# A recurrence of 64x64 products: units of two head groups, four quarters of the array, and outputs turned 128x128

## The chip, the cores and the metric

The kernel runs on one core of a Trainium2 chip. Its time is device microseconds (us) of one execution, the median of several runs. In what follows PE is TensorE's matmul side and PEld its weight loads; DVE is VectorE, ACT ScalarE, POOL GpSimd, SP SyncE, whose queue issues most DMAs.

## What is computed

The reference is two transformer blocks over 256 tokens of width 2048, all in float32. The first is an attention and convolution mixer with a gated feed-forward layer; the second has an "even" layer (another attention and a pooling branch) and an "odd" layer. The change touches the odd layer, and the first microseconds of the program.

The odd layer is a recurrence with a matrix state per head (32 heads of width 64):

```python
def step(state, inp):
    r_t, w_t, k_t, v_t, kk_t, a_t = inp
    sa = jnp.einsum('bhvk,bhk->bhv', state, -kk_t)
    state = (state * w_t[:, :, None, :]
             + sa[..., None] * (kk_t * a_t)[:, :, None, :]
             + v_t[..., None] * k_t[:, :, None, :])
    return state, jnp.einsum('bhvk,bhk->bhv', state, r_t)
```

Its inputs r, w, k, v, kk and a come from products of the shifted and mixed tokens with 2048x2048 weights (`od_w_r`, `od_w_k`, `od_w_v`) and two low-rank pairs. What it gives out is normalised per head, gets a bonus term, is multiplied by silu of a fourth product (`od_w_g`), and goes through `od_w_o`; a layer norm follows.

## The kernel before

Every large product streams its weights from HBM in pieces of 512 KB (`split_w`): one DMA on SP's queue into one of four buffers `wraw`, a ScalarE copy rounds it to the high part `wh` (L149), VectorE subtracts to get the low part `wl` (L151), and TensorE makes three products of high and low parts. `ws` (L168 to L170) has the tokens as the moving side, 24 matmuls of 256 columns a piece; `ts` (L187 to L189) has the weights moving, 12 matmuls of 512 columns a piece. Up to three pieces are fetched and split ahead.

After each piece `tick` is called. It takes items from queues that `spread` has filled, at a rate of items by ticks, so that all smaller work goes into the instruction streams between the pieces. When the program is built, a scheduler puts each engine's instructions into their final order from this order and the dependences, so that a step may move past a neighbour; `issue_after` adds an edge that it keeps. On the chip each engine takes its stream in order.

The recurrence is done in chunks of 64 tokens. The 32 heads are four groups j of eight heads; a group's pair index p (four pairs) and half h2 (two) name a head, with half h2 on partitions 0 to 63 or 64 to 127 (`HALF`). One `unit(j, c)` is one group and one chunk, 16 in all, each a list of steps which `slots` puts at places relative to a time t, the even and the odd group one place apart:

- `load_rows`: four DMAs of POOL's queue bring the factors from the spill in DRAM (L1343, tile `unit`); `load_values`: two of ACT's queue.
- `gram` (L1360): eight products with 64 rows, 128 columns, 128 moved columns, then two masking multiplies on VectorE (L1362).
- `pre`: eight 32x32 products (L1373) for the inverse of a triangular 64x64 block, and eight 64x64 products with the values (L1381).
- `join` (L1390): eight more 32x32 products; and the bonus on POOL (L1396).
- `seq_s` (L1404): eight 64x64 products with the state, where there is one (not in the first chunk).
- `seq_u`: four 128x128 transposes (L1412, copied by ScalarE, L1414; not in the last chunk), and eight 64x64 products that solve (L1417).
- `seq_o`: products that update the state (L1426, not in the last chunk) and that give the output (L1436, and L1440 with the state); four ScalarE copies bring the output out of PSUM (L1446).
- `norm`, `norm2`: the head norm, on ScalarE, VectorE and POOL (powers in `rpow`).

All these products are plain float32, which the profile shows as two records each. A step of one group is one PSUM bank of a ring of four (`aux`); it is emitted as pairs p with h2 inside, with the output half fixed by h2:

```python
PAIRS = [(h2, HALF[h2], HALF[1 - h2], p) for p in range(4) for h2 in range(2)]
...
for h2, hs, os, p in PAIRS:
    nc.tensor.matmul(ps[hs, p], st["ar"][hs, p, col[h2]], S[hs, p], start=True, stop=True)
```

The partitions of the operands choose the rows of the array and those of the output its columns, so this step uses two quarters of the 128x128 array, rows 0 to 63 with columns 0 to 63 and rows 64 to 127 with columns 64 to 127. Steps with `os` for one side use the two crossed quarters.

The queue of slots starts with the fourth v product, runs through the 32 pieces of the g products, and ends in the first half of the o products. Ahead of it, during the k products, `k_post` prepares each group's factors; its `blocks` (L1181) makes 16 64x64 products a call, in two calls a group, and `store_m` writes the masked 32x32 blocks to DRAM. `inverse` inverts them on VectorE, and `load_inverses` brings them back (L1320, tiles `xn`), four DMAs a group on SP's queue. `output(k)` turns the recurrence's output back with four transposes of 64-row pieces (L1504) for each of 16 tiles k.

At the program's start `mixer` builds six of the 16 token tiles (`to_fm`, transposes at L246, ScalarE copies at L316) before its first large product; the x pieces and the first weight pieces alternate on SP's queue.

Of the kernel before, what the change touches and what calls it, by code (L numbers as in the profile page):

```python
# [8 lines left out]
F32 = mybir.dt.float32  # L9
# [5 lines left out]
P = 128  # L15
# [22 lines left out]
class Mega:  # L38
# [116 lines left out]
    def ws(self, W, col0, X, evac):  # L155
# [110 lines left out]
    def constants(self):  # L266
# [9 lines left out]

        src = a["vecs"]
# [77 lines left out]
    def mixer(self):  # L355
# [537 lines left out]
    def odd(self, normed):  # L893
# [209 lines left out]
        def k_post(j, kr, kk, first):  # L1103
# [71 lines left out]
            def blocks(cp):  # L1175
                def go():
                    ps = self.aux().rearrange("p (u s) -> p u s", u=8)
                    for u in range(8):
# [3 lines left out]
                    st["mt", cp] = mt = kp.tile([P, 8, CH], F32, tag="mt", name="mt", bufs=2)  # L1182
                    nc.vector.tensor_tensor(out=mt, in0=ps, in1=gmask[:, 0, 0:CH].unsqueeze(1).broadcast_to((P, 8, CH)),
                                            op=ALU.mult)
                return go


            def store_m(cp):
                def go():
                    for h2 in range(2):  # L1190
                        for b in range(2):
                            o = h2 * 64 + b * 32
                            nc.sync.dma_start(
                                out=md[j // 2][j % 2, h2, b, cp * 8:cp * 8 + 8].rearrange("u s t -> s u t"),
                                in_=st["mt", cp][o:o + 32, :, b * 32:b * 32 + 32])
# [16 lines left out]
            def store_b():  # L1212
# [5 lines left out]
                    put(1, 0, lambda: st["r"]), put(0, 0, lambda: st["at"]), gains_k, blocks(0),  # L1218
                    put(0, 1, lambda: kk), row_k, blocks(1), wait, store_m(0), store_m(1)], [bonus, last, store_b]
# [82 lines left out]
        def r4(tag, name, shape=(4, CH), bufs=4):  # L1302
            return rp.tile([P, *shape], F32, tag=tag, name=name, bufs=bufs)

        def bank(n=CH):
            return self.aux()[:, :4 * n].rearrange("p (u s) -> p u s", s=n)

        def bc4(x):
            return x.unsqueeze(2).broadcast_to((P, 4, CH))


        PAIRS = [(h2, HALF[h2], HALF[1 - h2], p) for p in range(4) for h2 in range(2)]
        state = [None] * NG
# [9 lines left out]
        def unit(j, c):  # L1323
# [5 lines left out]
            def load_rows():  # L1329

                with self.tc.issue_after(seen["k"].ins):
                    load_factors()

            def load_factors():
                w = g8([P, 2048], "unit")
                st["ar"] = w[:, 0:512].rearrange("p (n s) -> p n s", n=4)
                st["bk"] = w[:, 512:1024].rearrange("p (n s) -> p n s", n=4)
                st["G"] = w[:, 1024:].rearrange("p (h n s) -> p h n s", h=2, n=4)

                d = w[:, 0:1024].rearrange("p (tn s) -> p tn s", s=P)  # L1340
                for h2, hs in enumerate(HALF):
                    for role in range(2):
                        nc.gpsimd.dma_start(  # L1343
                            out=d[hs, :, col[h2 ^ role]],
                            in_=spill[j][hs, c // 2, role].rearrange("p t n c s -> p (t n) c s")[:, :, c % 2])

            def load_values():

                st["Z"] = Z = r4("Z", "Z", (2, 4, CH))
                v = vall[c % 2 * CH:c % 2 * CH + CH, c // 2, j * 512:j * 512 + 512]  # L1350
                for h2 in range(2):
                    nc.scalar.dma_start(out=Z[HALF[1 - h2], h2],
                                        in_=v.rearrange("t (n h s) -> t h n s", n=4, h=2)[:, h2])

            def gram():
                ar, bk, G = st["ar"], st["bk"], st["G"]
                pss = [bank(P) for _ in HALF]
                for p in range(4):
                    for h2, hs in enumerate(HALF):
                        nc.tensor.matmul(pss[h2][:, p], bk[hs, p], ar[hs, p], start=True, stop=True)  # L1360
                for h2, ps in enumerate(pss):
                    nc.vector.tensor_tensor(out=G[:, h2], in0=ps, op=ALU.mult,  # L1362
                                            in1=gmask[:, h2].unsqueeze(1).broadcast_to((P, 4, P)))

            def pre():

                G, Z = st["G"], st["Z"]
                X = xn[j % 2][:, 4 * c:4 * c + 4]
                ps = bank(32)
                st["T"] = r4("Tm", "Tm", (4, 32), bufs=2)  # L1370
                for h2, hs, os, p in PAIRS:
                    o = 64 * h2
                    nc.tensor.matmul(ps[o + 32:o + 64, p], G[o:o + 32, h2, p, o + 32:o + 64], X[o:o + 32, p, 0:32],  # L1373
                                     start=True, stop=True)
                for o in (32, 96):
                    nc.vector.tensor_copy(st["T"][o:o + 32], ps[o:o + 32])
                st["X"] = r4("Xt", "Xt", bufs=2)
                nc.vector.transpose(st["X"].rearrange("p u s -> p (u s)"), X.rearrange("p u s -> p (u s)"))
                ps = bank()
                for h2, hs, os, p in PAIRS:  # L1380
# [349 lines left out]
```

## Time and profile before

| | before |
|---|---|
| median of 3 runs | 2441.2 us |
| lowest and highest run | 2435.44, 2445.77 us |
| profiled execution, its own time | 2436.61 us |
| its span in the profile | 2434.8 us |
| instructions | 39170 |
| PE, PEld, DVE, ACT, POOL busy | 2372.7, 2072.3, 1515.6, 1214.4, 223.4 us |
| TensorE clock granted, mean | 0.991 |
| HBM traffic over the span | 183 GB/s |

The span is that of one profiled execution, by the hardware profiler. Matmuls overlap in the records, so a busy PE is not one at its peak: the distance from one start to the next says what a matmul costs in a stream. A row "x16" of the timeline merges 16 records in a row; its first number is the first one's start, its second the time from there to the last one's end.

### The profile page before, as it was taken

To read this page: it belongs to the slowest core of one execution; us is meant where nothing else is said; L and a number is where in the kernel's file an instruction comes from. 1 tells how busy PE (TensorE), PEld (TensorE's weight loads), DVE (VectorE), ACT (ScalarE), POOL (GpSimd) and SP (SyncE) were. 2 spreads that over 40 slices of the span, in tenths; PEclk is the share of its full clock that TensorE was granted. 3 is DMA by queue.
4 is the path that set the end of the run, shared out by engine and by line. 5 is a ranking of instruction groups with operands and counts; after the bars stand their busy time and mean duration, and the time that the engine had idled before them with its cause. 6 is when DMAs were issued, how large, how long until landed. Compare 5 with 4: busy or idle time off the path is not lost.

```text
span 2434.8 us, 39170 instructions
## 1 busy us (share of the span) xinstructions
PE 2372.7 (97%) x15385; PEld 2072.3 (85%) x15385; DVE 1515.6 (62%) x2093; ACT 1214.4 (50%) x1937; POOL 223.4 (9%) x343
## 2 busy tenths in 40 slices
PE   8999999999999999999999999999999998999997
PEld 8998888788788888888888898999889996789975
DVE  5688888565654454454444544555587678885656
ACT  5433564444544444444344444564387765455662
POOL 0000200100000000000000000320000013145411
PEclk9999999999999999999999999999999999999998
DMA  7666656556566666666666556455666688866665
GB/s 230 196 185 192 175 170 189 160 185 203 160 191 190 190 190 185 191 191 190 193 194 191 168 184 190 149 164 182 196 189 194 185 238 232 220 169 157 149 169 135
DMA packets 287912, 451.18 MB, mean 185 GB/s; under 512 B 57903, under 2 KB 85103, under 8 KB 287727
## 3 DMA queue, kind: packets, MB, share of 16 engines
q1 hardware_dynamic: 263488, 428.50, 59.9%
q10 hardware_dynamic: 21167, 11.79, 1.8%
q0 software_dynamic: 3072, 8.39, 1.6%
q8 instruction: 121, 1.98, 0.3%
q14 instruction: 64, 0.52, 0.1%
HBM read 428.74 MB, written 17.77 MB: 183 GB/s over the span
## 4 chain that ended last, share of the span: by engine, by line
PE 78%; issue 7%; DVE 6%; DMA 4%; ACT 3%; POOL 1%; SPq 0%; ACTq 0%; DVEq 0%; POOLq 0%
PE acc L187 17%; PE acc L188 17%; PE acc L189 17%; PE acc L168 7%; PE acc L169 7%; PE acc L170 7%; DVE wl L151 2%; DMA wraw<-in_od_w_v 1%; ACT wh L149 1%; DMA wraw<-in_od_w_g 1%; DMA wraw<-in_od_w_k 0%; DMA inv<-md 0%; PE aux L246 0%; PE aux L659 0%; DVE xk L65 0%
## 5 line engine op out<-in xcount | busy, mean ns | idle before, releaser
L151 DVE TENSOR_TENSOR wl<-wraw,wh 128x1024 fp32r<-128x1024 f32 x762 | 935.1, 1228 | 752.8 <-ACT wh L149 750.0
L149 ACT ACTIVATE wh<-wraw 128x1024 fp32r<-128x1024 f32 x762 | 805.9, 1058 | 1004.4 <-PE acc L189 644.6
L187 PE MATMUL acc<-wh,xk 128*128 128x512 f32 x1520 | 599.6, 395 | 1.8 <-ACT kr L1226 1.3
L188 PE MATMUL acc<-wl,xk 128*128 128x512 f32 x1520 | 595.2, 392 | 5.4 <-DVE wl L151 5.3
L189 PE MATMUL acc<-wh,xk 128*128 128x512 f32 x1520 | 594.9, 391 | 0.0
L168 PE MATMUL acc<-xk,wh 128*128 128x256 f32 x1920 | 550.3, 288 | 0.5 <-ACT rr L1069 0.5
L169 PE MATMUL acc<-xk,wh 128*128 128x256 f32 x1920 | 544.5, 284 | 0.0
L170 PE MATMUL acc<-xk,wl 128*128 128x256 f32 x1920 | 540.8, 284 | 0.6 <-DVE wl L151 0.6
L168 PEld LDWEIGHTS acc<-xk,wh 128*128 128x128 f32 x1920 | 369.4, 193 | 4.4 <-ACT rr L1069 0.9
L169 PEld LDWEIGHTS acc<-xk,wh 128*128 128x128 f32 x1920 | 370.0, 193 | 0.4
L170 PEld LDWEIGHTS acc<-xk,wl 128*128 128x128 f32 x1920 | 367.5, 192 | 1.6 <-DVE wl L151 1.2
L188 PEld LDWEIGHTS acc<-wl,xk 128*128 128x128 f32 x1520 | 286.0, 188 | 65.3 <-DVE wl L151 7.5
L187 PEld LDWEIGHTS acc<-wh,xk 128*128 128x128 f32 x1520 | 285.9, 188 | 61.4 <-ACT kr L1226 1.5
L189 PEld LDWEIGHTS acc<-wh,xk 128*128 128x128 f32 x1520 | 286.1, 188 | 59.6
L187 PE MATMUL acc<-wh,f 128*128 128x512 f32 x352 | 139.1, 395 | 0.0
L188 PE MATMUL acc<-wl,f 128*128 128x512 f32 x352 | 138.9, 395 | 0.0
L189 PE MATMUL acc<-wh,f 128*128 128x512 f32 x352 | 138.9, 395 | 0.0
L427 DVE SCALAR_TENSOR_TENSOR slab<-zp,vec,slab 128x256 f32<-128x256 f32 x240 | 117.9, 491 | 4.2
L189 PEld LDWEIGHTS acc<-wh,f 128*128 128x128 f32 x352 | 66.3, 188 | 15.5
L187 PEld LDWEIGHTS acc<-wh,f 128*128 128x128 f32 x352 | 66.3, 188 | 15.5
L188 PEld LDWEIGHTS acc<-wl,f 128*128 128x128 f32 x352 | 66.3, 188 | 15.3
L725 POOL TENSOR_SCALAR_AFFINE_SELECT tri<-ones 128x128 f32<-128x128 f32 x1 | 0.3, 294 | 727.0 <-ACT junk L235 727.0
(318 smaller groups left out, 2149.1 us busy)
## 6 DMA issues: line engine op xcount, KB each, us to landing
wraw<-in_w_gate_up SPq DMA_DIRECT2D x176, 512.0 KB, 3.6
wraw<-in_w_in SPq DMA_DIRECT2D x144, 512.0 KB, 4.3
wraw<-in_ev_w_in SPq DMA_DIRECT2D x96, 512.0 KB, 3.6
wraw<-in_w_down SPq DMA_DIRECT2D x88, 512.0 KB, 4.7
wraw<-in_w_out SPq DMA_DIRECT2D x32, 512.0 KB, 4.2
wraw<-in_ev_w_out SPq DMA_DIRECT2D x32, 512.0 KB, 4.8
wraw<-in_od_w_r SPq DMA_DIRECT2D x32, 512.0 KB, 4.7
wraw<-in_od_w_k SPq DMA_DIRECT2D x32, 512.0 KB, 4.6
```

The costliest lines, as they stand in the source:

```text
L149: high = nc.scalar.activation(out=wh, in_=raw, func=AF.Copy)
L151: low = nc.vector.tensor_tensor(out=wl, in0=raw, in1=wh.bitcast(F32), op=ALU.subtract)
L168: nc.tensor.matmul(o, wh[:, kk, c], x[:, 0], start=k == 0, stop=False)
L169: nc.tensor.matmul(o, wh[:, kk, c], x[:, 1], start=False, stop=False)
L170: nc.tensor.matmul(o, wl[:, kk, c], x[:, 0], start=False, stop=k == kt - 1)
L187: nc.tensor.matmul(ps[t], x[:, 0, c], wh[:, kk], start=k == k1, stop=False)
L188: nc.tensor.matmul(ps[t], x[:, 0, c], wl[:, kk], start=False, stop=False)
L189: mm = nc.tensor.matmul(ps[t], x[:, 1, c], wh[:, kk], start=False, stop=k == k2 - 1)
L427: nc.vector.scalar_tensor_tensor(out=zc[:, n], in0=src, scalar=self.v1("w_dw", j * 8 + n), in1=zc[:, n], op0=ALU.mult, op1=ALU.add)
L725: nc.gpsimd.affine_select(out=tri, in_=self.ones, pattern=[[-1, P]], channel_multiplier=1, base=0, compare_op=ALU.is_ge, fill=0.0)
```

## The change

Six things change.

- A unit becomes two groups and one chunk, `unit(J, c)`, eight units in all. Steps are emitted for eight pairs; the output (or input) half now alternates with the pair (`ns`), so that the values' step, `seq_s` and `seq_u` go over all four quarters, into two banks by the pair's parity. The first 32x32 step goes to four tiles, the second stays on two. `gram` splits each product in two of 64 columns, over four quarters. The state update and the output keep their quarters.
- The slots are set anew: two Gram steps in two places, the transposes (`turn`) in one of their own, the second Gram place and the output step apart from the rest, `join` together with `seq_s`, and the first Gram place with `seq_u`.
- Because odd pairs need a block of the inverse in the other half, `load_inverses` has two more DMAs a group.
- `blocks` becomes one call a group, over four quarters and two banks; `store_m` writes with a stride of two.
- `output` turns two tiles at a time with four 128x128 transposes into one bank, read by the two calls.
- At the start four tiles instead of six are built ahead; the transposes of the later ones come after the first piece's matmuls, and a small ScalarE copy runs at once after the constants are set.

```diff
-                    nc.tensor.matmul(o, wl[:, kk, c], x[:, 0], start=False, stop=k == kt - 1)
+                    self.mm = nc.tensor.matmul(o, wl[:, kk, c], x[:, 0], start=False, stop=k == kt - 1)
...
+        nc.scalar.activation(out=self.sp1.tile([P, 16], F32, name="warm"), in_=self.mhalf, func=AF.Copy)
...
-            if k % 2 == 0 and k < 6:
+            if k in (0, 2):
                 self.x_piece(k // 2)
-            x = self.to_fm(k, "mix_pre_g")
-            if k % 2 and k < 6:
+
+            with self.tc.issue_after(self.mm.ins) if k >= 4 else ExitStack():
+                x = self.to_fm(k, "mix_pre_g")
+            if k in (1, 3):
                 with self.tc.issue_after(self.turned.ins):
                     self.fetch_w(k // 2 + 1)
+            if k == 3:
+                self.x_piece(2)
             return x
-        X = self.ahead(first_tile, 6, 0, fetch=piece)
+        X = self.ahead(first_tile, 4, 0, fetch=piece)
...
+                pss = [self.aux().rearrange("p (u s) -> p u s", u=8) for _ in range(2)]
+                for u in range(8):
+                    for e in range(2):
                         for h2, hs in enumerate(HALF):
-                            i = u % 4 * 4 + 2 * cp + u // 4
-                            nc.tensor.matmul(ps[hs, u], v64(kk)[hs, i], v64(st["at"])[hs, i], start=True, stop=True)
+                            i = (u % 2 * 2 + e) * 4 + u // 2
+                            nc.tensor.matmul(pss[e][HALF[h2 ^ e], u], v64(kk)[hs, i], v64(st["at"])[hs, i],
+                                             start=True, stop=True)
...
-        PAIRS = [(h2, HALF[h2], HALF[1 - h2], p) for p in range(4) for h2 in range(2)]
-        state = [None] * NG
+        PAIRS = [(h2, HALF[h2], HALF[1 - h2], HALF[h2 ^ p % 2], p) for p in range(8) for h2 in range(2)]
+        state = [None] * 2
...
+                o = 64 - h2 * 64
+                nc.sync.dma_start(out=xn[j % 2][o:o + 32, 1::2, 32:64],
+                                  in_=xd32[j // 2][j % 2, h2, 0, 1::2].rearrange("u s t -> s u t"))
...
+            def gram(j):
+                def go():
+                    pss = [bank(P, 4) for _ in HALF]
+
+                    for p in range(4):
+                        for h2, i in ((0, 0), (1, 1), (0, 1), (1, 0)):
+                            nc.tensor.matmul(pss[h2][HALF[i], p], bk(4 * j + p)[HALF[h2], col[i]],
+                                             ar(4 * j + p)[HALF[h2]], start=True, stop=True)
...
-                ps = bank()
-                for h2, hs, os, p in PAIRS:
-                    nc.tensor.matmul(ps[hs, p], G[os, h2, p, col[h2]], Z[os, h2, p], start=True, stop=True)
+                pss = [bank(u=4) for _ in HALF]
+                for h2, hs, os, ns, p in PAIRS:
+                    nc.tensor.matmul(pss[p % 2][ns, p // 2], G(h2, p)[os, col[h2]], Z[os, h2, p], start=True, stop=True)
...
-                ps = bank()
-                for h2, hs, os, p in PAIRS:
-                    nc.tensor.matmul(ps[hs, p], st["ar"][hs, p, col[h2]], S[hs, p], start=True, stop=True)
-                nc.vector.tensor_tensor(out=st["nv"], in0=ps, in1=st["nv"], op=ALU.add)
+                pss = [bank(u=4) for _ in HALF]
+                for h2, hs, os, ns, p in PAIRS:
+                    nc.tensor.matmul(pss[p % 2][ns, p // 2], ar(p)[hs, col[h2]], S[hs, p], start=True, stop=True)
+                for e, nv in enumerate(halves(st["nv"])):
+                    nc.vector.tensor_tensor(out=nv, in0=pss[e], in1=nv, op=ALU.add)
+
+            def turn():
+
+                if c == 3:
+                    return
+                st["bt"] = r8("bt", "bt", (8, P))
+                for j in range(2):
+                    ps = bank(P, 4)
+                    for p in range(4):
+                        nc.tensor.transpose(ps[:, p], bk(4 * j + p), self.ident)
+                    nc.scalar.activation(out=st["bt"][:, 4 * j:4 * j + 4], in_=ps, func=AF.Copy)
...
+                pss = [bank(u=4) for _ in HALF]
+                for h2, hs, os, ns, p in PAIRS:
+                    nc.tensor.matmul(pss[p % 2][hs, p // 2], st["X"][ns, p], st["nv"][ns, p], start=True, stop=True)
...
+            return [(load_rows, -6), (load_values, -6), (gram(0), -4), (gram(1), -3), (pre, -1), (join, 0), (seq_s, 0),
+                    (turn, 1), (seq_u, 2), (seq_o, 4), (norm, 6), (norm2, 8)]
...
-            for j in range(NG):
-                for c in range(4):
-
-                    t = 7 + 6 * (4 * (j // 2) + c) + j % 2
...
-                    for f, d in zip(u, (-6, -6, -4, -2, -1, 0, 2, 4, 6, 8)):
...
+            for n in range(8):
+
+                J, c, t = n // 4, n % 4, 6 + 6 * n
+                for f, d in early.get((J, c)) or unit(J, c):
...
-            ps, os = self.aux()[:, :T], HALF[1 - k % 2]
-            for c in range(4):
-                n = c // 2 * 32 + 8 * (k // 4) + c % 2 * 4 + k % 4 // 2 * 2
-                nc.tensor.transpose(ps[:, c * CH:c * CH + CH], ov[os, n:n + 2].rearrange("p n s -> p (n s)"),
-                                    self.ident[os, os])
+            if k % 2 == 0:
+                turned[k // 2] = ps = self.aux()
+                for c in range(4):
+                    n = c // 2 * 32 + 8 * (k // 4) + c % 2 * 4 + k % 4
+                    nc.tensor.transpose(ps[:, c * P:c * P + P], ov[:, n:n + 2].rearrange("p n s -> p (n s)"),
+                                        self.ident)
+            ps = turned[k // 2].rearrange("p (c h s) -> p c h s", c=4, h=2)[:, :, 1 - k % 2]
```

## Rows read from the trace of the kernel before

**Rows 1.** The page's first part: busy time of each engine.

```profile
PE 2372.7 (97%) x15385; PEld 2072.3 (85%) x15385; DVE 1515.6 (62%) x2093; ACT 1214.4 (50%) x1937; POOL 223.4 (9%) x343
```

**Rows 2.** Busy time by stretch: stretch, length, engines, granted clock, DMA share, GB/s.

```profile
1927.00:1980.00 53.00, 52.89 (x534) 52.12 (x534) 41.50 (x47) 32.50 (x47) 6.15 (x4) 1.00 0.77 219
2120.70:2316.40 195.70, 187.65 (x2717) 172.34 (x2712) 136.94 (x286) 119.12 (x391) 90.08 (x136) 0.98 0.65 160
2183.60:2190.40 6.80, 6.40 (x29) 6.21 (x29) 0.00 (x0) 2.32 (x5) 0.22 (x1) 0.50 0.47 141
```

**Rows 3.** PE's timeline near 2127 us: start, length, line, operands, count.

```profile
2126.29 0.60 PE L1412 MATMUL aux<-ident,unit 128*128 128x128 f32 x4
2126.82 0.68 PE L1417 MATMUL aux<-nv,Xt 64*64 64x64 f32 x16
2127.43 1.16 PE L1360 MATMUL aux<-unit 64*128 64x128 f32 x16
2128.52 0.39 PE L168 MATMUL acc<-xk,wh 128*128 128x256 f32 x1
2128.74 0.28 PE L169 MATMUL acc<-xk,wh 128*128 128x256 f32 x1
2128.86 0.27 PE L170 MATMUL acc<-xk,wl 128*128 128x256 f32 x1
```

**Rows 4.** PE's timeline near 2172 us, an output step and what follows.

```profile
2171.44 0.69 PE L1426 MATMUL aux<-Z,bt 128*64 128x64 f32 x16
2171.96 0.64 PE L1436 MATMUL aux<-Z,unit 128*64 128x64 f32 x16
2172.53 0.68 PE L1440 MATMUL aux<-S,unit 64*64 64x64 f32 x16
2173.14 0.44 PE L1373 MATMUL aux<-xn,unit 32*32 32x32 f32 x16
```

**Rows 5.** PE's timeline near 2148.5 us, two steps side by side.

```profile
2148.48 0.51 PE L1381 MATMUL aux<-Z,unit 64*64 64x64 f32 x10
2148.78 0.27 PE L1404 MATMUL aux<-S,unit 64*64 64x64 f32 x2
2148.82 0.28 PE L1381 MATMUL aux<-Z,unit 64*64 64x64 f32 x3
...
2148.95 0.51 PE L1404 MATMUL aux<-S,unit 64*64 64x64 f32 x11
```

**Rows 6.** PE's timeline near 1943 us, one call of `blocks`.

```profile
1943.09 1.15 PE L1181 MATMUL aux<-sq,kk 64*64 64x64 f32 x32
1944.16 0.38 PE L170 MATMUL acc<-xk,wl 128*128 128x256 f32 x1
```

**Rows 7.** PE's timeline near 2371 us, one output tile.

```profile
2370.94 0.46 PE L1504 MATMUL aux<-ident,h 64*128 64x64 f32 x4
2371.33 0.50 PE L187 MATMUL acc<-wh,xk 128*128 128x512 f32 x1
```

**Rows 8.** The timeline of all engines at the start, with idle time and releaser.

```profile
4.98 1.28 ACT L316 ACT_TABLE_LOAD   x1 [4.98 <-DVE vec L285]
...
7.11 1.12 PE L246 MATMUL aux<-ident,h 128*128 128x128 f32 x4 [1.68 <-DMA h<-in_x]
...
9.28 1.09 PE L246 MATMUL aux<-ident,h 128*128 128x128 f32 x4 [1.06 <-DMA h<-in_x]
...
10.02 0.56 PE L168 MATMUL acc<-xk,wh 128*128 128x256 f32 x1
...
10.60 0.41 PE L168 MATMUL acc<-xk,wh 128*128 128x256 f32 x1
```

**Rows 9.** PE's timeline near 2184 us, with idle time and releaser.

```profile
2184.00 2.04 PE L1360 MATMUL aux<-unit 64*128 64x128 f32 x8 [2.53 <-DMA unit<-spill]
```

**Rows 10.** SP's timeline near 2104 us: DMA issues.

```profile
2104.02 5.99 SPq L1320 DMA_DIRECT2D xn<-xi  x8
```

**Rows 11.** ACT's instruction groups from 2100 to 2375 us.

```profile
L1446 ACT ACTIVATE h<-aux 128x64 f32<-128x64 f32 x64 | 13.4, 223 | 13.6 <-PE aux L1440 10.6 <-PE aux L1373 1.5 <-PE aux L1436 1.3
```

More of the change, by code (lines that the diff above doesn't have):

```diff
@@ L1351, in load_values @@
+                v = vall[c % 2 * CH:c % 2 * CH + CH, c // 2, J * 1024:J * 1024 + 1024]
                 for h2 in range(2):
                     nc.scalar.dma_start(out=Z[HALF[1 - h2], h2],
[L1353 to L1363, printed above, removed]
@@ L1365, in pre @@
-            def pre():
[L1367 to L1370, printed above, removed]
-                for h2, hs, os, p in PAIRS:
[L1372 to L1378, printed above, removed]
-                ps = bank()
-                for h2, hs, os, p in PAIRS:
-                    nc.tensor.matmul(ps[hs, p], G[os, h2, p, col[h2]], Z[os, h2, p], start=True, stop=True)
-                st["nv"] = r4("nv", "nv", bufs=2)
-                nc.scalar.activation(out=st["nv"], in_=ps, func=AF.Copy)
+                                        in_=v.rearrange("t (n h s) -> t h n s", n=8, h=2)[:, h2])
@@ new lines, in pre @@
+            def pre():
+                Z = st["Z"]
+                st["T"] = r8("Tm", "Tm", (8, 32))
+                st["X"] = r8("Xt", "Xt")
+                pss = [bank(32, 4) for _ in HALF]
+                for h2, hs, os, ns, p in PAIRS:
+                    o, n, c1 = 64 * h2, ns.start, p % 2 * 32
+                    nc.tensor.matmul(pss[p % 2][n + 32:n + 64, p // 2], G(h2, p)[o:o + 32, o + 32:o + 64],
+                                     xn[p // 4][o:o + 32, 4 * c + p % 4, c1:c1 + 32], start=True, stop=True)
+                for e, t in enumerate(halves(st["T"])):
+                    for o in (32, 96):
+                        nc.vector.tensor_copy(t[o:o + 32], pss[e][o:o + 32])
+                for j in range(2):
+                    nc.vector.transpose(st["X"][:, 4 * j:4 * j + 4].rearrange("p u s -> p (u s)"),
+                                        xn[j][:, 4 * c:4 * c + 4].rearrange("p u s -> p (u s)"))
+                pss = [bank(u=4) for _ in HALF]
+                for h2, hs, os, ns, p in PAIRS:
+                    nc.tensor.matmul(pss[p % 2][ns, p // 2], G(h2, p)[os, col[h2]], Z[os, h2, p], start=True, stop=True)
+                st["nv"] = r8("nv", "nv")
+                for e, nv in enumerate(halves(st["nv"])):
+                    nc.scalar.activation(out=nv, in_=pss[e], func=AF.Copy)
@@ L1387, in join @@
                 ps = bank(32)
[L1388 to L1389 removed]
+                for h2, hs, os, ns, p in PAIRS:
+                    o = ns.start
                     nc.tensor.matmul(ps[o:o + 32, p], Tm[o + 32:o + 64, p], X[o + 32:o + 64, p, 32:64],
@@ L1407, in seq_u @@
             def seq_u():
                 Z = st["Z"]
-                if c < 3:
-                    ps = bank(P)
-                    for p in range(4):
-                        nc.tensor.transpose(ps[:, p], st["bk"][:, p], self.ident)
-                    st["bt"] = r4("bt", "bt", (4, P), bufs=2)
-                    nc.scalar.activation(out=st["bt"], in_=ps, func=AF.Copy)
-                ps = bank()
-                for h2, hs, os, p in PAIRS:
-                    nc.tensor.matmul(ps[hs, p], st["X"][hs, p], st["nv"][hs, p], start=True, stop=True)
@@ L1451, in norm @@
                 O, m = st["O"], st["m"]
-                v = self.sp.tile([P, 4], F32, tag="gv", name="gv", bufs=4)
-                for p in range(4):
+                v = self.sp.tile([P, 8], F32, tag="gv", name="gv", bufs=4)
+                for p in range(8):
                     sq = self.sp.tile([P, CH], F32, tag="sq", name="sq", bufs=2)
-                    nc.scalar.activation(out=sq, in_=O[:, p], func=AF.Square, bias=m[:, p:p + 1],
+                    nc.scalar.activation(out=sq, in_=O[:, p // 4, p % 4], func=AF.Square, bias=m[:, p:p + 1],
@@ L1465, in norm2 @@
-                nc.vector.tensor_tensor(out=O, in0=O, in1=gnw[:, 4 * j:4 * j + 4], op=ALU.mult)
-                nc.gpsimd.tensor_tensor(out=O, in0=O, in1=st["vb"], op=ALU.add)
-            return load_rows, load_values, gram, pre, join, seq_s, seq_u, seq_o, norm, norm2
+                for p in range(8):
+                    o = O[:, p // 4, p % 4]
+                    nc.scalar.activation(out=o, in_=o, func=AF.Identity, scale=r[:, p:p + 1], bias=m[:, p:p + 1])
+                pairs = lambda t: t.rearrange("p (j n) s -> p j n s", j=2)
@@ L1511, in output @@
             return x
-        early = {(j, c): unit(j, c) for c in range(2) for j in range(2)}
+        early = {(0, c): unit(0, c) for c in range(2)}
         for j in range(2, NG):
             if j == 2:
-                first = [f for u in early.values() for f in u[:2]]
+                first = [f for u in early.values() for f, _ in u[:2]]
                 first += [lambda h=h, f=f: f(h) for f in (load_bonus, load_gain) for h in range(2)]
```

132 lines of the change are left out of this document (72 added, 60 removed).

## The prediction

> **What bounds the kernel now.** I read the page first: TensorE (PE) is busy 97% of the span, VectorE 62%, ScalarE 50% [rows 1]. PE's busy time alone doesn't prove that PE sets the pace, so the table by stage came next. In the k products, in the long stretch with the g products and most of the recurrence, PE is busy 52.89 of 53.0 us and 187.65 of 195.7 us, while VectorE has 41.50 and 136.94 and the DMA share is 0.77 and 0.65 [rows 2]. There, a microsecond taken from PE is a microsecond of the end, until another wait shows. Then PE's timeline, to see what one step of the recurrence costs, and where two steps happened to stand side by side.
>
> How to read it: an fp32 product leaves two records, so a step of one group (eight products) is x16. A step's cost is the distance from its first start to the next row's first start. A 64x64 step costs 2127.43 - 2126.82 = 0.61 us, the turn of four 128x128 blocks 0.53, the Gram step 1.09 [rows 3]. With the length of one record (0.22 us) taken off, the 64x64 step's starts lie (0.68 - 0.22)/15 = 31 ns apart, 61 a product; the remaining 0.11 us is getting in and out. The large products run 0.12 us apart, but the first after a small shape takes 0.22 [rows 3]; with as much on the way in, a tick with odd shapes loses about 0.2 us beside the steps themselves.
>
> **Does a step in four quarters run faster?** Before, a 64x64 step uses two quarters of the array (row half h to column half h, or the two crossed ones). No step uses four. But at 2148 us two steps that use opposite pairs of quarters ran together: up to 2148.78 ten records of L1381 start in 0.30 us, and from then to 2148.95 eleven of L1381 and L1404 start (two and three in the rows shown, six in those left out), 15 ns apart [rows 5]. So each quarter seems busy for 4 x 31 = 123 ns a product, and four quarters halve the pitch. I take that.
>
> **The change, part by part** (n = 0 to 7 are the units of two groups and one chunk).
>
> *64x64 steps (values, state, solve).* Two groups cost 2 x 0.61 = 1.22; after, 32 records at 15 ns and 0.11 make 0.59; of the difference I take 0.61. 22 such steps (8 for the values, 6 with a state, 8 to solve): 22 x 0.61 = 13.4 us. If four quarters gave nothing, only one entry per step is saved: 22 x 0.11 = 2.5.
>
> *32x32 steps.* The pitch of L1373 is (0.44 - 0.19)/15 = 17 ns, the step about 0.37 [rows 4]. The first step goes to four tiles: 0.74 to 0.37, eight times, 3.0 us (only merged: 0.8). The join stays on two tiles, merely merged: 8 x 0.1 = 0.8.
>
> *Gram.* It becomes twice as many products, 64x64 with 128 moved columns; no row shows that shape. A quarter's 123 ns are two weight loads and two passes of 64 columns; with passes twice as long, 6 x 31 = 185, over four quarters 46 a product, 16 products and 0.11: 0.85 a group. Bounds: with only two products at a time 1.6 (a loss of 0.5), with long passes hidden 0.6 (a gain of 0.5). I take 0.85, since the mixing row is nearest; rounded, 0.25 off 1.09, 16 times: 4.0 us (-8 to +8).
>
> *State update and output.* Same quarters, same count. Now 0.52 + 0.57 + 0.61 = 1.70 a group [rows 4]; 96 records at 31 ns and 0.11 make 3.1 for two: 0.3 x 7 = 2.0 us.
>
> *Turn.* Eight 128x128 transposes alone in a tick have the large products' shape, so no switch: 0.53 to 0.44 for four, 12 times, 1.1 us; and eight ticks lose no 0.2: 1.6 us.
>
> *blocks.* 32 records cost 1.07 [rows 6], twice a group; after, 64 at 15 ns and 0.11 = 1.07 in all. 1.07 for the first three groups, 3.2 us; the fourth falls where weights are late, and is not counted (0 to 1.1).
>
> *Outputs.* Four 64x64 turns cost 0.39 [rows 7] and mostly 0.2 of switching; after, two outputs share four 128x128 turns (0.44) with no switch. 16 x 0.39 + some 10 x 0.2 = 8.2 to 8 x 0.44 = 3.5 would be 4.7; several already share a tick, so 3.5 us (2 to 5).
>
> *Start.* PE waits for the third piece of x at 9.28 before its first large product at 10.02, though the second four transposes are through at 8.23 [rows 8]. Now four tiles come first, not six: the first product can start at 8.2 to 8.4. The table load of 1.28 us, in the way of the first x tile, moves ahead of the data. 1.8 us earlier, but before the clock is up (a record of L168 takes 0.41 us there, 0.28 for L169 in mid-stretch [rows 3, 8]), so about half of that, and the two tiles' transposes, 1.09 there, run quicker later: 1.4 us (0.9 to 2.8).
>
> *What it adds.* Two more copies of inverses a group: the eight that SyncE issues at 2104 take 5.99 us [rows 10], so twelve take 9; the weight loads queue behind, three ahead of need at some 3 us each. I charge 1 us (0 to 6). Banks: four steps now take two banks each. The output bank is emptied by eight ScalarE copies, 8 x 13.4/64 = 1.7 us by their busy time [rows 11], at most 3.4 if reading each one's sum doubles that; the next step wants the bank after a chunk of 24 x 0.12 = 2.9 us. So nothing, or 0.5 x 7 = 3.6; I charge 1. VectorE, ScalarE and GpSimd move the same elements in fewer instructions, behind PE: 0 while PE is the limit.
>
> Sum: 13.4 + 3.0 + 0.8 + 4.0 + 2.0 + 1.1 + 1.6 + 3.2 + 3.5 + 1.4 - 2 = 32.0 us. The profiled execution took 2436.6, so 2404.6; the runs' median (2441.2) is 4.6 above it: **2409 us**.
>
> **Rivals.**
> *Only two products at a time.* Quarters that share rows or a bank take turns. Then (merged only) 2.5 + 0.8 + 0.8 - 8 + 2.0 + 2.7 + 0.3 + 3.5 + 1.4 - 2 = 4.0 us are left: 2437, or 2429 if Gram breaks even. For it: no step shows four quarters by itself. Against it: the mixed rows [rows 5]. The Trainium skill, TensorEngine Tiling (Restrictions and Gotchas, PSUM Pressure) states that different row tiles can't use one PSUM bank simultaneously. By that rule the new 64x64 steps, whose two banks each take both row halves, would run two at a time, and the time is this rival's. The trace leans against it: two row halves in one bank already run at 61 ns a product, where by my account of the mixed rows a lone quarter takes 123. The skill's TensorE: Matmul & The Clock Gate (Part 1, on the matmul gap) gives a floor of about 25 ns from start to start; by it, the 64x64 steps would gain some 7 us less and the end be 2416. The 17 and 15 ns seen here are below that floor, so I give it no case of its own.
>
> *Rows late (slower).* GpSimd now issues a unit's eight copies in one go, after the norm's powers and the bonus products in its queue, and the first Gram waits for them. One such wait stands in the trace: 2.53 us before L1360 [rows 9], followed by 6.8 us at clock 0.50 [rows 2], which costs 3.4 more. Six units load inside the recurrence: 6 x 5.9 = 35 us would eat the whole gain (2444); with waits of 4 us or more each (6 x 7.4 = 44) it is slower by over 0.5%. Against it: the buffer is released by the output step of unit n-2, four slots before the Gram of n, as before.
>
> *Waits that eat part.* Steps twice as wide leave twice the work to ScalarE and VectorE after each, and the steps come faster; a bank or a copy late by 1 to 2 us at two places of each unit costs 11 to 20 us: 2421 to 2429.
>
> **How the numbers follow.** Forecast 0.63, part eaten 0.14, two at a time 0.09, rows late 0.14 (0.03 of it within 0.5%). A measurement of this kernel can tell about 0.5% (12.2 us) from no change: 2429.0 and 2453.4 are the edges. Faster 0.63 + 0.14 = 0.77; same 0.09 + 0.03 = 0.12; slower 0.11. The forecast's own range: 2395 (Gram's better bound, the start's, and the wait and clock loss of 5.9 gone) to 2421 (Gram's worse bound and the charges' upper ends, in part). Reaching to 2431 takes in the eaten case and the better part of two at a time, and leaves out some 0.18.
>
> **What would show it.** Right: records of a 64x64 step 15 ns apart and the step of 32 about 0.6 us; a Gram step of 32 records at some 0.85; first large product at about 8.3 us; turns in a tick with no 0.22 us behind them; the stretch of the g products shorter by some 22 us. Wrong: pitches of 31 ns in four quarters; PE waiting on DMA at the Gram lines, on ScalarE at the values' step; new stretches at clock 0.5; or VectorE or SyncE becoming the last to release PE.

## The result, and the profile after

The changed kernel takes 2421.9 us (2420.4 to 2423.9, 4 runs) against 2438.4 (2435.4 to 2445.8) of the kernel before beside it: a ratio of 0.9928, 95% interval 0.9912 to 0.9945. It is faster by 16.5 us, where 32 were forecast from the profiled execution. The profiled execution has a span of 2422.1 us, 12.7 less than before's, so 19 us of the sum are missing between the two traces. In all fences below PE's new lines are: 1189 the blocks, 1387 Gram, 1402 and 1422 the two 32x32 steps, 1412 values, 1439 state, 1458 solve, 1451 the turn, 1469, 1479 and 1483 state update and output, 1549 the outputs' turns; 1462 is VectorE's copy of the solution `Z`, 151 its subtraction `wl` for the weight split, and 1581 ScalarE's silu of the g products, the gate. (In the two kernels with two quarters the lines from 1384 on stand three lower.)

The page's first part, to be held against [rows 1]:

```profile
PE 2350.3 (97%) x15609; PEld 2056.3 (85%) x15609; DVE 1515.0 (63%) x2059; ACT 1209.9 (50%) x1938; POOL 210.3 (9%) x287
```

PE is busy 22.4 us less. The steps themselves came out nearly as forecast. PE's timeline of the changed kernel (start, length, line, operands, count), each row against [rows 3], [rows 4] or [rows 6]:

```profile
1939.95 1.16 PE L1189 MATMUL aux<-sq,kk 64*64 64x64 f32 x64
1941.04 0.39 PE L170 MATMUL acc<-xk,wl 128*128 128x256 f32 x1
...
2220.74 0.46 PE L1402 MATMUL aux<-xn,unit 32*32 32x32 f32 x32
2221.12 0.69 PE L1412 MATMUL aux<-Z,unit 64*64 64x64 f32 x32
2221.75 0.38 PE L168 MATMUL acc<-xk,wh 128*128 128x256 f32 x1
...
2232.23 0.69 PE L1458 MATMUL aux<-nv,Xt 64*64 64x64 f32 x32
2232.74 1.05 PE L1387 MATMUL aux<-unit 64*64 64x128 f32 x32
2233.73 0.39 PE L168 MATMUL acc<-xk,wh 128*128 128x256 f32 x1
...
2341.36 0.60 PE L1549 MATMUL aux<-ident,h 128*128 128x128 f32 x4
2341.72 0.48 PE L187 MATMUL acc<-wh,xk 128*128 128x512 f32 x1
```

A 64x64 step of two groups takes 0.51 to 0.63 us from its start to the next, 32 records some 15 ns apart: (0.69 - 0.22)/31. The first 32x32 step takes 0.38, Gram 0.99 a group, the blocks 1.09, two outputs' turns 0.36.

So where are the missing 19 us? The windows of the changed kernel (stretch, length, busy time of each engine, granted clock, DMA share, GB/s), the whole recurrence first, then the stretches at half clock in it:

```profile
2105.00:2302.00 197.00, 177.69 (x2881) 162.41 (x2881) 135.80 (x260) 110.63 (x372) 79.76 (x90) 0.94 0.70 166
2169.90:2180.10 10.20, 7.62 (x57) 6.85 (x58) 2.75 (x5) 4.67 (x13) 2.26 (x2) 0.50 0.69 189
2210.90:2214.30 3.40, 3.40 (x21) 3.26 (x16) 2.31 (x5) 0.68 (x2) 0.00 (x0) 0.50 0.38 129
2238.20:2241.60 3.40, 3.40 (x18) 3.40 (x17) 2.09 (x5) 0.00 (x0) 0.11 (x1) 0.50 0.31 110
2289.40:2296.20 6.80, 5.41 (x26) 5.41 (x27) 5.06 (x11) 0.81 (x2) 1.77 (x1) 0.50 0.63 154
```

PE is idle for 19.3 of 197 us, where it was 8.05 of 195.7 [rows 2]; and 23.8 us lie at 1.2 GHz instead of 2.4, against 10.2 before (the 6.8 of [rows 2], and 3.4 at 2115 us). 11.3 us more idleness and, at half speed, some 7 us of lost clock: that is nearly all that is missing. So the 32 pieces of the g products, whose stretch the prediction had some 22 us shorter, take nearly as long as before: 185.3 us from their first product to the first of the o products (2119.9 to 2305.2), 187.9 before (2128.5 to 2316.4). Most of what was gained lies ahead of them: some 5.5 us in the two products before v and in v, and 3 in the first feed-forward layer (below). The waits of PE in the same stretch of the changed kernel (waited for: us, times, longest) say for what:

```profile
PE aux L1387 <- DVE Z L1462: 7.8, 7, 3.1
PE aux L1549 <- DVE Z L1462: 3.6, 1, 3.6
PE acc L168 <- ACT gate L1581: 1.6, 1, 1.6
PE aux L1387 <- DMA unit<-spill: 1.3, 2, 0.9
PE aux L1458 <- DVE nv L1441: 1.1, 1, 1.1
```

In the kernel before, the same two steps waited for that copy for 1.2 us in all:

```profile
PE aux L1504 <- DVE Z L1419: 0.8, 2, 0.4
PE aux L1360 <- DVE Z L1419: 0.4, 1, 0.4
```

Neither Gram nor an output's turn reads that copy of `Z` there. What they want is its source: the solve's two banks. There are four auxiliary banks. In one slot the solve of a unit takes two and the first Gram step of the next unit the other two, so the second Gram step, a slot later, can start only when VectorE has copied the solution out. The timelines of VectorE, GpSimd and PE of the changed kernel around 2288 us show why that copy is late:

```profile
2285.93 1.28 POOL L1510 TENSOR_TENSOR h<-h,vb 128x512 f32<-128x512 f32 x1 [5.29 <-DVE h L1509]
2286.08 4.19 DVE L151 TENSOR_TENSOR wl<-wraw,wh 128x1024 fp32r<-128x1024 f32 x2 [0.23 <-ACT wh L149]
2287.29 1.90 POOL L1429 TENSOR_TENSOR vb<-Z,bsum 64x512 f32<-64x512 f32 x1
2288.21 2.06 DVE L151 TENSOR_TENSOR wl<-wraw,wh 128x1024 fp32r<-128x1024 f32 x1
2289.27 1.90 POOL L1429 TENSOR_TENSOR vb<-Z,bsum 64x512 f32<-64x512 f32 x1
2290.31 0.77 DVE L1462 COPY Z<-aux 64x256 f32<-64x256 f32 x2
2290.79 1.11 PE L1549 MATMUL aux<-ident,h 128*128 128x128 f32 x4 [3.62 <-DVE Z L1462]
```

The solve ended at about 2286.2, but two subtractions stand ahead of the copy in VectorE's order (the x2 row holds both, the second again by itself), and each takes over 2.0 us where one alone takes 1.23. PE sits 3.62 us, and the clock halves for 6.8 us from 2289.4 on, while it still sits.

### The profile page after: what moved, and what is told of

The parts are those of the page before. It is cut to its first block, busy times and chain, and to the rows that moved or that the text cites. A ratio compares the mean times of both kernels' runs of the same rounds, so it can differ in the third digit from the quotient of the medians.

```text
span 2422.1 us, 39486 instructions
## 1 busy us (share of the span) xinstructions
PE 2350.3 (97%) x15609; PEld 2056.3 (85%) x15609; DVE 1515.0 (63%) x2059; ACT 1209.9 (50%) x1938; POOL 210.3 (9%) x287
## 4 chain that ended last, share of the span: by engine, by line
PE 78%; issue 8%; DVE 6%; ACT 4%; DMA 3%; POOL 1%; SPq 0%; DVEq 0%; ACTq 0%; POOLq 0%
PE acc L187 18%; PE acc L189 17%; PE acc L188 17%; PE acc L168 7%; PE acc L169 7%; PE acc L170 6%; DVE wl L151 2%; ACT wh L149 1%; DMA wraw<-in_od_w_v 1%; DMA wraw<-in_od_w_k 1%; PE aux L665 0%; PE aux L1387 0%; DVE inv L1266 0%; DVE inv L1268 0%; DMA wraw<-in_w_in 0%
## 5 line engine op out<-in xcount | busy, mean ns | idle before, releaser
L169 PE MATMUL acc<-xk,wh 128*128 128x256 f32 x1920 | 546.9, 285 | 0.8 <-DVE xk L319 0.8
L169 PEld LDWEIGHTS acc<-xk,wh 128*128 128x128 f32 x1920 | 372.6, 194 | 1.2 <-DVE xk L319 1.2
```

## The experiments

The theory: the banks. The rivals: VectorE is late whatever the banks; the clock falls because of the small shapes themselves; the units' rows come late. Times of the timed kernels, each compared with the kernel before on the same chip (whose medians there were 2436.6 to 2438.4). Differences in the text are between the medians of the first column, some of them of different chips; by the ratios they come out up to 1.6 us otherwise.

| kernel | us | ratio to before (95%) |
|---|---|---|
| changed | 2421.9 | 0.9928 (0.9912 to 0.9945) |
| first Gram step a slot earlier | 2408.9 | 0.9878 (0.9860 to 0.9896) |
| solution copied by ScalarE | 2414.9 | 0.9902 (0.9886 to 0.9918) |
| both | 2408.8 | 0.9881 (0.9867 to 0.9894) |
| rows a slot earlier only | 2418.2 | 0.9918 (0.9905 to 0.9932) |
| no bonus products | 2419.2 | 0.9920 (0.9904 to 0.9936) |
| two quarters | 2426.7 | 0.9954 (0.9937 to 0.9971) |
| two quarters, Gram earlier | 2417.2 | 0.9913 (0.9899 to 0.9926) |
| old start | 2426.5 | 0.9952 (0.9939 to 0.9966) |
| Gram earlier, denser inversion | 2413.3 | 0.9899 (0.9883 to 0.9916) |
| the same, bonus split | 2411.9 | 0.9895 (0.9881 to 0.9910) |
| Gram earlier, gate beside inverse | 2401.1 | 0.9851 (0.9827 to 0.9874) |

**The first Gram step a slot earlier.**

```diff
-            return [(load_rows, -6), (load_values, -6), (gram(0), -4), (gram(1), -3), ...
+            return [(load_rows, -7), (load_values, -6), (gram(0), -5), (gram(1), -3), ...
...
-                    if (J, c) in early and d < -4:
+                    if (J, c) in early and d < -5:
```

> The first Gram step of a unit goes one slot earlier, into the slot of the 128x128 turn, and the unit's rows are loaded one slot earlier with it, so that no slot fills all four auxiliary banks with a solve and a Gram step, and the solve's two banks are wanted again two slots later instead of one. Theory of the banks (the gain was lost because the next Gram step or output turn waits for the solve's two banks, which VectorE frees late): the waits of the Gram step and of the output turn on the copy of the solution, 11.4 us in the changed kernel, fall below 4, the stretches at a granted clock of 0.5 in the recurrence from 24 us to at most 14, and the time by 8 to 12 us, to 2410 to 2414. Rival, VectorE is late whatever the banks: the waits move to the next reader of a VectorE result and the time stays within 3 us of 2422. Rival, the clock falls because of the small products themselves: the waits go, the 0.5 stretches stay, and 4 to 6 us are gained.

It took 2408.9, 13.0 less than the changed kernel and a little more than the 8 to 12 expected. PE's waits in the same microseconds of this kernel, the longest four:

```profile
PE acc L168 <- ACT gate L1581: 1.9, 1, 1.9
PE aux L1451 <- ACT bt L1452: 1.8, 1, 1.8
PE aux L1451 <- DVE Xt L1425: 1.1, 1, 1.1
PE aux L1412 <- DVE S L1474: 1.0, 1, 1.0
```

and its windows:

```profile
2105.00:2302.00 197.00, 188.78 (x3104) 172.14 (x3103) 144.15 (x276) 124.89 (x414) 80.58 (x95) 0.96 0.71 172
2166.20:2179.90 13.70, 11.36 (x105) 10.21 (x106) 6.11 (x10) 6.24 (x16) 0.81 (x1) 0.50 0.57 170
```

No wait on `Z` is left; idleness fell from 19.3 to 8.2 us. The stretches at half clock only went from 23.8 to 17.1 us, slightly more than was expected; 13.7 of them are one stretch, taken up below. The pieces of the g products take 171.0 us here, 14.3 less than in the changed kernel. The gain is mostly the waits, so the theory of the banks holds, and the small shapes as such aren't what costs the clock: at 2228 us the same steps run without a fall.

**The solution copied by ScalarE.**

```diff
-                    nc.vector.tensor_copy(u[1][HALF[1]], pss[e][HALF[1]])
+                    nc.scalar.activation(out=u[1][HALF[1]], in_=pss[e][HALF[1]], func=AF.Copy)
```

> The second half of the solve is copied out by ScalarE instead of VectorE, so that the two banks come free without passing VectorE's queue; nothing else changes. Theory of the banks with a late VectorE: the same waits vanish as with the Gram step moved, and 6 to 11 us are gained (2411 to 2416). Rival, ScalarE is as late as VectorE (its own queue of weight copies and gates): the waits stay under the name of ScalarE, within 3 us of 2422. Rival, the clock falls by the small products alone: 4 to 6 us gained and the stretches at 0.5 stay.

2414.9, 7.0 less, with the order of Gram and rows untouched: the release of the banks alone is worth that. The waits on `Z` fell from 11.4 to 2.6 us, now on ScalarE, but a wait of 5.9 us for ScalarE's first gate came in (1.6 in the changed kernel):

```profile
PE acc L168 <- ACT gate L1581: 5.9, 1, 5.9
PE aux L1387 <- ACT Z L1462: 2.1, 4, 1.0
PE aux L1549 <- ACT Z L1462: 0.5, 1, 0.5
```

**Both.** The edits are the two above.

> Both cures together: the first Gram step a slot earlier, and the second half of the solution copied by ScalarE. If both worked on one and the same wait, as the theory of the banks says, the second adds nothing: 2407 to 2410, as with the Gram step alone. If VectorE's work itself was too much in the recurrence (rival), the two add: 2400 to 2404.

2408.8: the second cure adds nothing to the first. It is one wait, seen from its two ends.

**Rows a slot earlier only** (`(load_rows, -7)`, Gram as in the changed kernel).

> A control for the Gram step's move, which also loaded the rows of a unit one slot earlier: here only that, the Gram step stays. Theory of the banks: at most the 1.3 us of the Gram step's waits on the rows are gained, 2420 to 2422, and the waits on the copy of the solution stay near 11 us. Rival, the rows were what came late: 8 us or more gained.

2418.2, 3.7 less; I had expected 2 at most. The waits on the rows are gone, those on `Z` went from 11.4 to 7.1 us:

```profile
PE aux L1387 <- DVE Z L1462: 4.7, 7, 2.5
PE aux L1549 <- DVE Z L1462: 2.4, 1, 2.4
```

So a part of the 13.0 may belong to the rows; how far 3.7 us can be told from a chance shift of this stage is taken up at the end.

**No bonus products** (line 1429 left out, the bonus term is missing from the output; the addition after the norm adds the gain tile instead).

> Leaves out the bonus products on GpSimd (two of 1.9 us a unit); the last addition takes the norm's gain tile in the place of their result, so its work is the same. Theory that VectorE is late because its weight subtractions run beside GpSimd's products: the subtractions of 2.06 to 2.2 us fall to about 1.3 in the recurrence, the waits on the copy of the solution halve, and 4 to 8 us are gained (2414 to 2418). Rival, VectorE's order alone sets the wait: the subtractions get shorter but the waits stay, less than 3 us gained.

2419.2, 2.7 less: the rival's bound. The subtractions in the stretch fell from a mean of 1403 to 1330 ns (1227 before the change), the waits on `Z` from 11.4 to 8.7. GpSimd's products make the copy later; they aren't the main cause that it is waited for. GpSimd's addition (L1510) stayed, so what it alone does to the copy isn't shown.

**Two quarters.**

```diff
-        PAIRS = [(h2, HALF[h2], HALF[1 - h2], HALF[h2 ^ p % 2], p) for p in range(8) for h2 in range(2)]
+        PAIRS = [(h2, HALF[h2], HALF[1 - h2], HALF[h2], p) for p in range(8) for h2 in range(2)]
...
-                            nc.tensor.matmul(pss[e][HALF[h2 ^ e], u], v64(kk)[hs, i], v64(st["at"])[hs, i],
+                            nc.tensor.matmul(pss[e][HALF[h2], u], v64(kk)[hs, i], v64(st["at"])[hs, i],
...
-                    o, n, c1 = 64 * h2, ns.start, p % 2 * 32
+                    o, n, c1 = 64 * h2, ns.start, 0
```

(and without the two extra copies in `load_inverses`).

> Undoes one part: every 64x64 and 32x32 product goes to the half of the output rows of its head, so that a step runs over two quarters of the array as before the change, with all other steps, shapes and slots kept; the two extra loads of inverse blocks go too. Theory of the prediction: a record's pitch goes from 15.4 to about 31 ns, 0.5 us for each of the 22 steps of 32 records (values, state, solve), 0.3 to 0.5 for the 16 steps of 32x32 products, 1.0 for each of the four block steps: some 20 us more TensorE time. If all of it lies on the path: 2440 to 2443. If the waits for VectorE in the recurrence cover a part: 2428 to 2438. Rival, the pitch does not change by the quarters: within 3 us of 2422.

2426.7, 4.8 more, below the 2428 to 2438 expected. PE's timeline of this kernel: a first 32x32 step, a values step, a solve, a call of `blocks`:

```profile
1941.82 2.08 PE L1189 MATMUL aux<-sq,kk 64*64 64x64 f32 x64
1943.83 0.39 PE L170 MATMUL acc<-xk,wl 128*128 128x256 f32 x1
...
2162.45 0.69 PE L1399 MATMUL aux<-xn,unit 32*32 32x32 f32 x32
2163.08 1.15 PE L1409 MATMUL aux<-Z,unit 64*64 64x64 f32 x32
2164.16 0.39 PE L168 MATMUL acc<-xk,wh 128*128 128x256 f32 x1
...
2235.35 1.09 PE L1455 MATMUL aux<-nv,Xt 64*64 64x64 f32 x30
...
2236.34 1.04 PE L1384 MATMUL aux<-unit 64*64 64x128 f32 x30
```

Twice the pitch, as the prediction had it: the values step 1.08 against 0.63, the solve 0.99 against 0.51, the 32x32 step 0.63 against 0.38, the blocks 2.01 against 1.09. That is 22 x 0.46 + 8 x 0.25 + 4 x 0.92 = 16 us of PE, of which 4.8 reach the end. Without the wait for the banks:

**Two quarters, Gram a slot earlier.**

> The Gram step a slot earlier, and every 64x64 and 32x32 product over two quarters of the array only. With the banks full, four quarters were worth 4.8 us (2426.7 against 2421.9) of some 14 us that TensorE is longer busy. If waits for VectorE covered the rest, it shows now that they are gone: 8 to 15 us over the 2408.9 of the Gram step alone, 2417 to 2424. Rival, that the rest is covered by waits which the Gram step's move does not touch: again 3 to 6 us, 2412 to 2415.

2417.2, 8.3 over the 2408.9: now a good half of the 16 us shows. But PE also waits 6.4 us for the first gate here, 1.9 without:

```profile
PE acc L168 <- ACT gate L1578: 6.4, 1, 6.4
```

so up to 4.5 of the 8.3 may be that wait and not the steps themselves.

**Old start** (six tiles ahead, no early copy).

> The changed kernel with the start of before: no early ScalarE copy, six tiles turned ahead instead of four. The prediction's theory: the new start is worth 1.4 us, so 2423.5. What the two traces say: the new start has the first large product 2.2 us earlier but loses this again in the first chunks, and is 0.6 us behind at 200 us: then the time falls by 0.6, to 2421.3; either way inside 1.5 us of the changed kernel, and the place to read is the start of the first large product after 190 us. Besides: the down products of the first feed-forward layer, whose code is the same, took 388 ns in the changed kernel and 395 before, 3.4 us in all. If it hangs on where tiles lie after the one small tile that the early copy adds, they are 395 here; if not, 388.

2426.5, 4.6 more than the changed kernel in the medians, where at most 1.5 either way was expected. The trace tells two parts. At the same large product at 199 us (1536 large products in, the same in all kernels) the old start is 0.4 us ahead. In the first feed-forward layer's down products it loses some 3 us: groups of one line and shape, busy time and mean ns, in the old start's kernel

```profile
L188 PE MATMUL acc<-wl,f 128*128 128x512 f32 x352 | 138.9, 395 | 0.0
```

and in the changed kernel

```profile
L188 PE MATMUL acc<-wl,f 128*128 128x512 f32 x352 | 136.7, 388 | 0.0
```

The other two lines of these products, 187 and 189, went from 395 to 394 and 392 ns; the three together are 3.4 us. Yet the two profiled executions end level (2424.0 and 2423.9): this one got the 3 us back in the recurrence, with 13.6 us at half clock instead of 23.8. So no trace shows where the 4.6 of the medians lie.

**The kernel before with the early copy alone** (one line of the change).

> The kernel before with one line of the change: the early ScalarE copy of 16 columns into a small tile of its own. It is run to be read at the down products of the first feed-forward layer, 395 ns a record before and with the old start, 388 in every kernel with the new start. If the copy, or the tile that it adds, is the cause: 388 here. If the order of the first tiles is the cause: 395. The table load should stand near 1.3 us, and the first large product near 8 to 10 us.

388 ns in line 188 and some 3 us less at those products too: the copy or its 16-column tile does it, not the order of tiles. Which of the two wasn't told apart. Its first large product starts at 9.69 us, 0.3 earlier than before; the rest of the 2.2 us goes with the four tiles. In its one execution (2439.2 us) the recurrence took some 6 us longer than in before's profiled one, though nothing in it was changed, with 20.4 us at half clock instead of 10.2. So this stage can differ by that much with the same code in it. That the shift of the beginning did it isn't shown: executions of the kernel before alone lie between 2432.2 and 2445.8.

**Denser inversion** (`len(iq) / 2.5` instead of 2.3), on the kernel with the Gram step moved. What is left there is the stretch of 13.7 us at half clock: ScalarE's first gate waits 4.85 us for the store of the second inverse, whose buffer the gate tile takes.

> The Gram step a slot earlier, and the items of the two inversions spread over 8% fewer ticks, so that the store of the second inverse lands before the first gate tile, which takes its buffer, is written. In the kernel with the Gram step alone ScalarE sat 4.85 us until that store had landed, TensorE 1.9 us behind it, and a stretch of 13.7 us at a clock of 0.5 lay there (2166 to 2180 us). If the store's landing holds the path: the wait goes and 2 to 8 us are gained on 2408.9. Rival: TensorE is held there by the solve's chain on VectorE anyway, and the denser inversion takes back elsewhere what is gained: within 2 us of 2408.9.

2413.3, 4.4 more, which neither theory had. VectorE's last column ended only 2.5 us earlier (2163.1 against 2165.6); the store was issued right behind it, as it had been, and landed 11.9 us later instead of 7.5, so the gate came later than without. (The next expectation but one puts the late issue down to the weight loads on SyncE's queue; these times show that it was the column.) ScalarE's wait grew to 9.2 us:

```profile
ACT L1581 <- DMA xi<-inv: 9.2, 1, 9.2
```

**The bonus sums in two items**, on top of that.

> As the kernel with the earlier inverse, and the bonus sums of the key stage in two items, the product on VectorE one tick ahead of the turns that TensorE makes of it; in the kernel with the Gram step alone TensorE waited 3.6 us there for the product and the clock lay at 0.5 for 6.8 us just before and after it. If that wait is on the path: 3 to 6 us less than with the earlier inverse alone. Rival: the weights set the pace in that stage (VectorE and ScalarE hand TensorE its split weights with waits of 0.3 to 0.9 us each), and the wait comes back there: within 2 us of it.

2411.9, 1.4 less, the rival's answer: PE still waits 3.3 us there for the product, and the clock falls as before.

**The gate beside the inverse.** The inverse moves to the last third of its buffer, and the first eight gate tiles into the other two.

```diff
-                    m, x, w = (st["t"][:, n] for n in range(3))
+                    m, w, x = (st["t"][:, n] for n in range(3))
...
-        gates = [pp.tile([P, 8, T], F32, tag="xg", name="gate"), rp.tile([P, 8, T], F32, name="gate2")]
-        gk = [gates[k // 8][:, k % 8] for k in range(KT)]
+        gate2 = rp.tile([P, 8, T], F32, name="gate2")
+
+        def gk(k):
+            if k >= 8:
+                return gate2[:, k - 8]
+            return inv_tile[1][:, 0:2].rearrange("p n s t -> p (n s t)")[:, k * T:k * T + T]
```

> The Gram step a slot earlier, and the first eight gate tiles lie in the two thirds of the second inversion's buffer that hold its input and its scratch, beside the inverse itself, so that the first gate waits for VectorE's last column and not for the landing of the store. The denser inversion did not reach this: its store was issued only 2.1 us earlier, behind weight loads on the same queue, and landed 11.9 us later instead of 7.5. If the store's landing holds the path: ScalarE's 4.85 us and TensorE's 1.9 us of waiting at 2170 us go, and with a shorter stretch at a clock of 0.5 2 to 6 us are gained on 2408.9. Rival: TensorE is held there by the recurrence's chain on VectorE: the wait moves, and the time stays within 2 us of 2408.9.

2401.1 (2397.9 to 2405.5), 7.8 under the Gram step alone (6.6 by the ratios), more than the 2 to 6 expected, and the fastest of all: a ratio of 0.9851 to before. Its windows, the recurrence and the one stretch at half clock that is left in it:

```profile
2105.00:2302.00 197.00, 190.30 (x3164) 172.77 (x3164) 147.73 (x281) 127.19 (x418) 79.40 (x95) 0.99 0.75 182
2173.40:2176.80 3.40, 3.40 (x19) 3.40 (x18) 1.46 (x3) 1.67 (x6) 1.38 (x2) 0.50 0.93 347
```

The gate's wait is gone from PE, the pieces of the g products take 164.4 us, 6.7 us of idleness are left, and the clock is 0.99 where the changed kernel had 0.94. What had held TensorE here was once more a buffer: the gate wanted the store's place, not its result.

## Why the prediction was right and wrong

The time (2421.9) is in the range and the direction is right, but the likeliest case was not it: of the 32 us of the sum about half arrived, which is the rival "waits that eat part" (2421 to 2429). Two of the prediction's own signs of being wrong came: new stretches at clock 0.5, and VectorE releasing PE.

- **64x64 steps**: right. 15 ns and 0.51 to 0.63 us for two groups, as 0.61 was taken; two quarters give 30 ns, 31 taken. "Only two products at a time" falls. The rule of TensorEngine Tiling (Restrictions and Gotchas, PSUM Pressure) in the Trainium skill, which gives that rival's time, isn't borne out by these rows: each of the step's two banks takes both row halves, and yet the records follow at half the pitch of two quarters.
- **32x32 and blocks**: right (0.38 for 0.37; 1.09 for 1.07). **Outputs**: 0.36 for four turns, 0.44 taken. **State update and output**: 3.09 for 3.1.
- **Gram**: mis-sized. 0.99 a group, not 0.85, so of 4.0 us some 16 x 0.14 = 2.2 are missing.
- **Start**: mis-sized. The first large product came 2.2 us earlier (7.80), but at 199 us the kernel was 0.6 us behind before, not 1.4 ahead. The first chunk ran wholly at the low clock, two more tiles were turned among the products, and PE waited 0.85 us at 24.7 us for VectorE's tile (L169). The early copy brought some 3 us at another place that no row pointed to.
- **Banks**: this is the step that failed. "So nothing, or 0.5 x 7 = 3.6; I charge 1" looked only at the output step's bank. The solve's two banks, with Gram's two in the same slot, cost 11.4 us of waits (1.2 before), and 13.6 us at half clock begin within 1.4 us of the end of three of them, as much as was added in all. With the Gram step moved those waits are gone, but 17.1 us at half clock are left elsewhere. Of the rivals, "waits that eat part" had named this, a bank or a copy late, and was given 0.14. The later sentence of the same part failed with it: "behind PE: 0 while PE is the limit". Once a bank is the link, VectorE's order is on the path.
- **"A microsecond taken from PE is a microsecond of the end"**: held only in part. 16 us of PE were worth 4.8 with the banks full and 8.3 at most with them free.
- **Rows late**: 1.3 us of waits in the trace, up to 3.7 us by the run; far from the 35 priced.

With the Gram step moved the time is 2408.9, the 2409 of the forecast. That is partly chance, as the start and Gram were off, and the copy's 3 us were not in the sum.

What stays open: single differences of 2.7 to 4.8 us (no bonus products, rows earlier, old start, two quarters with the banks full) are no larger than the 6 us by which the unchanged recurrence differed between two executions, so their shares aren't settled. The 13.0, 7.0 and 7.8 us are each seen in the waits that went with them; of the 8.3, 4.5 may be a wait for the gate. Why the store of the denser inversion took 11.9 us to land isn't known. Whether the solve could write to one bank from all four quarters wasn't tried.

## What to carry to other kernels

When a step is merged to twice its width, count for each slot of the schedule how many banks it takes, which engine empties them, and what stands ahead of that copy in the engine's order; the ring makes a step wait for a bank whose data it never reads. Moving one step to a slot with free banks (and the loads it needs with it) gave 13.0 us, where the whole change had given 16.5. And look at who else wants a buffer: a store's landing can hold the next writer of its tile, and then giving the writer other room does what hurrying the store did not.

## What the hardware showed that was not expected

VectorE's subtraction and GpSimd's two-input operations took turns. Undisturbed, the subtraction took 1.23 us, and GpSimd's product 1.04 (at 2179 us). At 2286 us GpSimd's addition ran from 2285.93 to 2287.21; the subtraction that began at 2286.08 ended 1.07 us after it, GpSimd's next product (1.90 us, begun at 2287.29) 0.9 us after that subtraction, and so on: each is over about one undisturbed duration after the other's end. The Trainium skill's SBUF — State Buffer (section on the two separate sides) says of VectorE operations with two SBUF inputs and GpSimd operations that read SBUF that they hold a shared port pair as an exclusive lock for the whole instruction; the rows agree.

The down products' records of 512 columns took 395 ns in all three lines or 394, 388 and 392 ns in the same code, depending on one small copy at the program's start. No run here shows why.
